# A streaming-encoder block on one core: up pairs 13, 15 and 17 in seven-product steps, the sums of x read on GpSimd's queue, and two edits at the ends of the up phases

## The chip, the cores and the metric

The kernel runs on one core of a Trainium2 chip. That core has five engines that work at once: TensorE (PE in the profile, with its weight loads as PEld), VectorE (DVE), ScalarE (ACT), GpSimd (POOL) and SyncE (SP). SP, ACT and POOL each have a queue for DMA transfers. The metric is the device time of one execution in microseconds; the median of several runs is compared.

## The reference

One layer of a hybrid encoder on x of 512 tokens by 1024 features, in float32. The change touches only the channel mixing part, the up and the down projection; in the reference it reads

```python
h = rms_norm(x, norm_ffn_g[l])
u = causal_dwconv(h @ w_up[l], conv_ffn_w[l])     # 1024 -> 2 x 2816, three taps
a, b = jnp.split(u, 2, axis=-1)
x = x + (jax.nn.silu(a) * b) @ w_down[l]          # 2816 -> 1024
```

In front of it stand the input projection, a gated convolution, attention with a forget gate, and their merge; behind it a last norm. None of these is changed.

## The kernel before

**Arithmetic.** TensorE multiplies numbers of a rounded kind. To keep float32's accuracy each factor is held as a high part, the rounded copy, and a low part, what the rounding left. A product is then three matmuls: high by high, low weight by high x, high weight by low x. The low parts of the weights are `wl`, the high ones `wh`; of activations the names are `x1h`/`x1l` (the input of the up projection, each 128 features by 512 tokens in eight blocks) and `gh`/`gl` (256 tokens wide, for everything that is summed first).

**Weights.** A list `stream` holds all weight chunks in the order of their use. For each chunk SP issues a load (L182) into one of four raw buffers, ACT copies it to `wh` (`split`, L275), DVE takes the difference `wl` (L279), and TensorE uses both. `wh` and `wl` have two buffers each, so the split of a chunk waits until TensorE is done with the chunk before the last. ACT and DVE run their instructions strictly in program order: whatever stands in front of a split delays it.

**Up pairs.** The 5632 columns of the up projection are 44 blocks of 128; block 2j and 2j + 1 are the pair j, the two factors of the gate. Pairs 0 to 11 are phase 0, 12 to 21 phase 1. A plain pair takes two chunks `up` and 96 matmuls. A pair in `SUP` is done with seven products instead of eight for each 2 x 2 block of blocks (Strassen's scheme in Winograd's form). It takes two steps; each has a chunk P (three products that use weights as they are, 18 matmuls) and a chunk F (four products with sums of weights, 24 matmuls). The sums of weights are formed in DRAM by DMA alone: SP copies (L208), POOL's queue adds with an accumulating DMA (L211). The sums of x lie in `gh`/`gl` too. In phase 0 DVE and ACT make them and store their float32 form to DRAM (`ys`). Since `gh`/`gl` hold other things at the end of phase 0, phase 1 reads that form back in four quarters y10 to y13 (`up_forms`: DMA at L1084, `gh` on ACT at L1076, `gl` on DVE at L1079). The tile `y` has one buffer: the read of a quarter is issued when the `gl` of the quarter before is done.

**Behind an up pair.** DVE multiplies the result by the norm (L1171), ACT and DVE apply the three taps (L566, L567, L570), ACT applies SiLU (L1231), POOL or DVE multiplies the two factors (`ge` for even pairs at L1236, `go` for odd ones), and after an odd pair DVE forms sums and ACT and DVE their high and low parts (L1262, L1263), the input of the down projection.

**Down steps.** At the end of each phase the down projection of that phase's pairs follows, again in seven-product steps (`STEPS`) with chunks P and F.

**What sets the order.** The Python program writes the engines' instructions in one order, and each engine keeps it. Work of ACT and DVE that may wait is put in a list `later`, each entry with the number of the chunk at whose split it is due, an estimate of its time, and tags ("e": evaluation of an up pair; "q": sums for the down steps). `split` ends with `run_later`, which writes out what is due, as far as its time fits; `flush_only` writes out everything with a tag at once. At the last pair of each phase `up` calls both.

Of the kernel before, what the change touches and what calls it, by code (L numbers as in the profile page):

```python
# [42 lines left out]
PHASES = ((0, 12), (12, NP))  # L43
# [4 lines left out]
STEPS = (  # L48
    tuple(((i, q), (i, q + 1)) for i, q in ((0, 0), (0, 2), (1, 0), (1, 2), (0, 4), (1, 4)))
    + tuple(((i, q), (i, q + 1)) for i in (3, 2) for q in (0, 2, 4)),  # L50
    (((2, 6), (2, 7)), ((2, 8), (2, 9)), ((0, 6), (0, 7)), ((0, 8), (2, 10)), ((0, 9), (0, 10)))
    + (((1, 6),), ((1, 7), (1, 8)), ((1, 9), (1, 10))),
)

# [3 lines left out]
PLAIN = [(m, k) for m in (6, 7) for k in range(*PHASES[1])]  # L58
PCUTS = (0, 8, 12, 20)

SUP = ((1, 2, 5), (14, 16))
XF = (26, 0)
UPD = tuple(tuple(((j, q), (j, q + 1)) for j in js for q in (0, 2)) for js in SUP)
DOUBLES = GATES + UPD[0] + STEPS[0] + UPD[1] + STEPS[1]
# [6 lines left out]
def block_kernel(ctx, tc, xT, vecs, wv, win, wmix, wo, wup, wst, wdp, outT):  # L71
# [3 lines left out]
    nc = tc.nc  # L75
# [6 lines left out]
    def keep(ins):  # L82
        return tc.keep_in_program_order(ins)
# [72 lines left out]
    later = []  # L156
# [638 lines left out]
    for i in range(n + LA):  # L795
# [8 lines left out]
        if 0 <= i - LA < n:  # L804
            pr, e, qb = units[i - LA]
# [249 lines left out]
    def up_forms(q, ph):  # L1055

        y = (gx if ph or q % 2 else hp).tile([P, 4, 2 * P], F32, tag="y", name=f"y{ph}{q}")
        b11, b12, b21, b22 = (y[:, i, :] for i in range(4))
        fs = slice(XF[ph] + 4 * q, XF[ph] + 4 * q + 4)

        def scale():
            for b in range(2):
                kb = 2 * q + b
                nc.scalar.activation(
                    y[:, 2 * b : 2 * b + 2, :], x1[:, kb, :].rearrange(halves_of, h=2), AF.Copy, scale=col(G2 + kb)
                )
            nc.vector.tensor_sub(b11, b11, b12)
            nc.vector.tensor_sub(b12, b22, b12)

        def sums():  # L1070
            nc.vector.scalar_tensor_tensor(b22, b11, -1.0, b22, op0=ALU.mult, op1=ALU.subtract)
            nc.vector.scalar_tensor_tensor(b21, b22, -1.0, b21, op0=ALU.mult, op1=ALU.subtract)


        def parts_of():
            nc.scalar.activation(gh[:, fs, :], y, AF.Copy)  # L1076
            if not ph:
                keep(nc.scalar.dma_start(ys[q], y))
            nc.vector.tensor_sub(gl[:, fs, :], y, gh.bitcast(F32)[:, fs, :])  # L1079
            if ph and q < 3:  # L1080
                up_forms(q + 1, ph)

        if ph:
            keep(nc.sync.dma_start(y, ys[q]))  # L1084
            due = [c[0] for c in stream].index(f"F{ND[0] + len(STEPS[0]) - 2}") + q
            later.append((due, 0.85, (("x", q),), parts_of))
            return
        for f, us in ((scale, 0.85), (sums, 0.85), (parts_of, 1.25)):
            later.append((0, us, (("x", q),), f))
# [51 lines left out]
    def up(j, ph, rb2, pu=None):  # L1141
        uu = []

        def tap(i, z):
            u = fp.tile([P, S], F32, tag="fu", name=f"fu{j}{i}", bufs=3)
            taps(u, z, CF + 3 * (2 * j + i))
            uu.append(u)

        if j in SUP[ph]:
            c = 2 * SUP[ph].index(j)  # L1150
            slot()
            seven(
                UPD[ph][c : c + 2], NU[ph] + c, {j: USETS[j]}, lambda q, g: up_form(ph, q, g), of="x",
                done=lambda i, banks, ids: merge(ph, j, banks, ids, rb2, tap, uu),
            )
            slot()
            return
        evacs = []
        for i in range(2):
            slot()  # L1160
            p = pu[i] if pu else block(f"up{2 * j + i}", x1h, x1l, True)
            if i and j + 1 == PHASES[ph][1]:
                split_next()
                if any(("e",) in w[2] for w in later):
                    flush_only((("e",),))
                    split()
            z = [None]

            def mul(i=i, p=p, z=z):
                z[0] = fp.tile([P, S], F32, tag="fz", name=f"fz{j}{i}", bufs=4)  # L1170
                nc.vector.tensor_mul(z[0], p, rb2)  # L1171

            evac = [(0.7, mul), (1.4, lambda i=i, z=z: tap(i, z[0]))]
            if i:
                evac.append((0, lambda: glu(ph, j, uu)))
            if any(("e",) in w[2] for w in later):
                later.extend((0, us, (("e",), acc.last) if x == 0 else (("e",),), f) for x, (us, f) in enumerate(evac))
            else:
                for _, f in evac:
                    f()  # L1180
# [46 lines left out]
    def glu(ph, j, uu):  # L1227
        a, b = uu
        q, k = j // 2, len(parts) - 1
        g0 = place(ph, q)  # L1230
        nc.scalar.activation(a, a, AF.Silu)  # L1231
        if j == NP - 1:
            nc.scalar.activation(tbl, a[: 4 * H, :1], AF.Sqrt, scale=0.0, bias=eps[: 4 * H])
        if j % 2 == 0:
            ge = glu.even = fp.tile([P, 2, 2 * P], F32, tag="ge", name=f"ge{q}", bufs=2)
            keep(nc.gpsimd.tensor_mul(ge, a.rearrange(halves_of, h=2), b.rearrange(halves_of, h=2)))  # L1236
            return
        flush_only([("q", x) for x in range(q)])
        ge = glu.even
        go = fp.tile([P, 6, 2 * P], F32, tag="gr", name=f"go{q}")  # L1240

        def mul(eng):
            return eng.tensor_mul(go[:, 0:2, :], a.rearrange(halves_of, h=2), b.rearrange(halves_of, h=2))

        if j + 1 < PHASES[ph][1]:
            keep(mul(nc.gpsimd))
        else:
            later.append((k + 3, 0.7, (("q", q),), lambda: mul(nc.vector)))
        b11, b12 = ge[:, 0, :], ge[:, 1, :]
        b21, b22, t1, t2, t3, t4 = (go[:, i, :] for i in range(6))  # L1250

        def t13():
            nc.vector.tensor_sub(t1, b11, b12)
            nc.vector.tensor_sub(t3, b22, b12)

        def t24():
            nc.vector.scalar_tensor_tensor(t2, t1, -1.0, b22, op0=ALU.mult, op1=ALU.subtract)
            nc.vector.scalar_tensor_tensor(t4, t2, -1.0, b21, op0=ALU.mult, op1=ALU.subtract)

        def hl(src, gs):  # L1260
            def f():
                nc.scalar.activation(gh[:, gs, :], src, AF.Copy)  # L1262
                nc.vector.tensor_sub(gl[:, gs, :], src, gh.bitcast(F32)[:, gs, :])  # L1263

            return f


        d = (2, 3, 4) if j + 1 < PHASES[ph][1] else (4, 5, 6)
        w = [(d[0], 0.85, t13), (d[0], 0.85, t24), (d[1], 0.7, hl(ge[:, : 1 + ph, :], slice(g0, g0 + 1 + NF * ph, NF)))]
        w += [(d[x > 0 and 2 or 1], 0.7, hl(go[:, x : x + 2, :], slice(g0 + 1 + x, g0 + 3 + x))) for x in (0, 4, 2)]  # L1270
        at = next((x for x, i in enumerate(later) if ("e",) in i[2]), len(later))
        later[at:at] = [(k + n, us, (("q", q),), f) for n, us, f in w]
# [49 lines left out]
    X, Y = (6, 7, 0, 1), (2, 3, 4, 5)  # L1322
    for ph, (j0, j1) in enumerate(PHASES):
        if ph:
            acc = turns(*(6, 7, 0, 1) * 4)
            make_forms(ND[1], len(DOUBLES), ph)
        for j in range(j0, j1):
            pu = None
# [208 lines left out]
```

## Time and profile before

| | |
|---|---|
| time, median of 3 runs | 694.92 us (694.84 to 695.49) |
| profiled execution | 694.18 us, of which the span of the trace is 692.4 us |
| granted TensorE clock, mean | 0.997 |
| phase 0, down steps | 465.8 to 523.8 us |
| phase 1, up pairs 12 to 21 | 523.8 to 631.1 us |
| phase 1, down steps | 631.1 to 667.8 us |
| plain end | to 692.4 us |

Stage bounds are the starts of the first matmuls of the stages in the timeline. A row of a timeline reads: start and duration in us, engine, line of the program, operation, what is written and read (buffer numbers left out), shape, count, and in brackets how long the engine stood idle before it and what ended the wait. A letter q behind an engine's name is its DMA queue.

### The profile page before, as it was taken

Reading aid. Unit: us, or ns where it says so; the run is one execution under the profiler, and the core shown is the slowest. Engines: PE = TensorE matmul, PEld = TensorE weight load, DVE = VectorE, ACT = ScalarE, POOL = GpSimd, SP = SyncE. Lnnn points to the kernel's source line nnn. Section 1 sums busy time; section 2 is a strip of 40 time slices with the busy share of each in tenths; the row PEclk is TensorE's granted clock in tenths of the full one; section 3 lists DMA queues with packets and bytes.
Section 4 is the critical chain, followed back from the end, with each engine's and each line's share of the span. In section 5 each row is a group of like instructions: output and inputs, shape, how many; then the busy total and the mean of one; then the engine's idle time right before and its main releaser. Section 6 shows DMA issues by size and latency. Waiting matters only on the chain. (4 is left out here: it accounts for less than half of the span.)

```text
span 692.4 us, 14690 instructions
## 1 busy us (share of the span) xinstructions
PE 683.1 (99%) x5936; PEld 680.6 (98%) x5936; DVE 554.2 (80%) x858; ACT 368.3 (53%) x579; POOL 190.5 (28%) x201
## 2 busy tenths in 40 slices
PE   9999999999999999999999999999999999999996
PEld 9999999999999999999999999999999999999995
DVE  6677787877578778769879699998787899988894
ACT  5675755554554444546554555545444544545572
POOL 6134947542020201214400144340100325231000
PEclk9999999999999999999999999999999999999998
DMA  8629999552568586788998498888945996676413
GB/s 308 225 67 293 216 243 204 134 120 92 185 144 221 166 268 205 230 308 213 158 313 241 126 233 222 200 242 231 252 149 167 337 231 157 188 168 182 154 31 122
DMA packets 65012, 137.53 MB, mean 199 GB/s; under 512 B 5760, under 2 KB 30352, under 8 KB 64688
## 3 DMA queue, kind: packets, MB, share of 16 engines
q1 hardware_dynamic: 44664, 107.28, 47.2%
q0 software_dynamic: 18464, 26.03, 23.4%
q10 hardware_dynamic: 1816, 3.29, 1.3%
q8 instruction: 46, 0.75, 0.4%
q14 instruction: 22, 0.18, 0.1%
HBM read 132.31 MB, written 47.71 MB: 260 GB/s over the span
## 5 line engine op out<-in xcount | busy, mean ns | idle before, releaser
L211 POOL DMA_DIRECT2D f<-in_wst_dram x66 | 77.7, 1371 | 27.1 <-DMA f<-f 26.8
L309 PE MATMUL p_up<-x1h,wh_up 128*128 128x256 f32 x416 | 81.2, 276 | 0.0
L309 PE MATMUL p_up<-x1l,wh_up 128*128 128x256 f32 x416 | 81.0, 276 | 0.0
L309 PE MATMUL p_up<-x1h,wl_up 128*128 128x256 f32 x416 | 81.0, 276 | 0.0
L279 DVE TENSOR_TENSOR wl_F<-raw_F,wh_F 128x1024 fp32r<-128x1024 f32 (+1 forms) x42 | 55.9, 1330 | 20.0 <-ACT wh_F L275 20.0
L275 ACT ACTIVATE wh_F<-raw_F 128x1024 fp32r<-128x1024 f32 (+1 forms) x42 | 44.3, 1054 | 39.5 <-PE dn L327 28.7
L309 PEld LDWEIGHTS p_up<-x1h,wh_up 128*128 128x128 f32 x416 | 62.7, 188 | 0.0
L309 PEld LDWEIGHTS p_up<-x1l,wh_up 128*128 128x128 f32 x416 | 62.7, 188 | 0.0
L309 PEld LDWEIGHTS p_up<-x1h,wl_up 128*128 128x128 f32 x416 | 62.6, 188 | 0.0
L309 PE MATMUL p_in<-xgh,wh_in 128*128 128x256 f32 x288 | 56.8, 279 | 0.0
L309 PE MATMUL p_in<-xgh,wl_in 128*128 128x256 f32 x288 | 56.6, 278 | 0.0
L309 PE MATMUL p_in<-xgl,wh_in 128*128 128x256 f32 x288 | 56.5, 278 | 0.0
L279 DVE TENSOR_TENSOR wl_P<-raw_P,wh_P 128x768 fp32r<-128x768 f32 (+1 forms) x42 | 41.7, 992 | 14.7 <-ACT wh_P L275 8.6
L327 PE MATMUL dn<-gh,wh_F 128*128 128x256 f32 x216 | 51.2, 277 | 1.2 <-ACT wh_F L275 1.2
L275 ACT ACTIVATE wh_P<-raw_P 128x768 fp32r<-128x768 f32 (+1 forms) x42 | 35.1, 835 | 32.1 <-PE dn L327 23.2
L327 PE MATMUL dn<-gl,wh_F 128*128 128x256 f32 x216 | 51.0, 276 | 0.0
L1236 POOL TENSOR_TENSOR ge<-fu,fu 128x512 f32<-128x512 f32 x11 | 20.1, 1831 | 110.5 <-DVE fu L570 85.6
L279 DVE TENSOR_TENSOR wl_up<-raw_up,wh_up 128x1024 fp32r<-128x1024 f32 x34 | 43.8, 1288 | 7.4 <-ACT wh_up L275 7.4
L275 ACT ACTIVATE wh_up<-raw_up 128x1024 fp32r<-128x1024 f32 x34 | 35.8, 1054 | 19.4 <-PE p_up L309 9.3
L309 PEld LDWEIGHTS p_in<-xgh,wh_in 128*128 128x128 f32 x288 | 44.7, 188 | 0.7
L309 PEld LDWEIGHTS p_in<-xgl,wh_in 128*128 128x128 f32 x288 | 43.7, 188 | 0.0
L309 PEld LDWEIGHTS p_in<-xgh,wl_in 128*128 128x128 f32 x288 | 43.6, 188 | 0.0
(343 smaller groups left out, 2211.8 us busy)
## 6 DMA issues: line engine op xcount, KB each, us to landing
raw_F<-f SPq DMA_DIRECT2D x41, 512.0 KB, 5.7
raw_up<-in_wup_dram SPq DMA_DIRECT2D x34, 512.0 KB, 5.6
raw_P<-in_wst_dram SPq DMA_DIRECT2D x41, 384.0 KB, 5.4
raw_in<-in_win_dram SPq DMA_DIRECT2D x24, 512.0 KB, 3.6
f<-in_wst_dram POOLq DMA_DIRECT2D x41, 256.0 KB, 6.8
f<-in_wst_dram SPq DMA_DIRECT2D x20, 512.0 KB, 7.1
f<-in_wst_dram POOLq DMA_DIRECT2D x20, 512.0 KB, 9.1
f<-f SPq DMA_DIRECT2D x40, 256.0 KB, 6.5
```

The source lines that it names most:

```text
L211: return lambda: keep(nc.gpsimd.dma_start(dst, src, accum_op=ALU.add))
L275: ins = nc.scalar.activation(hi, raw, AF.Copy)
L279: ins = nc.vector.tensor_sub(lo, raw, hi.bitcast(F32))
L309: keep(nc.tensor.matmul(out[:, cs], w, x[:, cs], start=start and i == 0 and c == 0, stop=stop and i == 2 and c == len(cut) - 1,))
L327: keep(nc.tensor.matmul(out, wl if x == 1 else wh, xl if x == 2 else xh, start=opens and bk not in seen, stop=closes and bk not in left,))
L1236: keep(nc.gpsimd.tensor_mul(ge, a.rearrange(halves_of, h=2), b.rearrange(halves_of, h=2)))
```

## The change

Pairs 13, 15 and 17 of phase 1 are done in seven-product steps in place of 14 and 16: one pair more, and all of them odd. The four reads of the sums of x go through POOL's queue in place of SP's. The down step of phase 1 that did positions (0, 8) and (2, 10) together is cut in two of one position each. At the last pair of each phase a split is now made always, and in front of what is flushed, where it was made behind it. The due numbers of the sums of a pair are one later if the next pair is a seven-product one, which concerns pair 1 alone. The turn of the PSUM banks of phase 1 follows.

```diff
@@ STEPS
-    (((2, 6), (2, 7)), ((2, 8), (2, 9)), ((0, 6), (0, 7)), ((0, 8), (2, 10)), ((0, 9), (0, 10)))
+    (((2, 6), (2, 7)), ((2, 8), (2, 9)), ((0, 6), (0, 7)), ((0, 8),), ((2, 10),), ((0, 9), (0, 10)))
@@
-SUP = ((1, 2, 5), (14, 16))
+SUP = ((1, 2, 5), (13, 15, 17))
@@ up_forms
         if ph:
-            keep(nc.sync.dma_start(y, ys[q]))
+            keep(nc.gpsimd.dma_start(y, ys[q]))
@@ up
             if i and j + 1 == PHASES[ph][1]:
                 split_next()
-                if any(("e",) in w[2] for w in later):
-                    flush_only((("e",),))
-                    split()
+                split()
+                flush_only((("e",),))
@@ glu
-        d = (2, 3, 4) if j + 1 < PHASES[ph][1] else (4, 5, 6)
+        d = (4, 5, 6) if j + 1 == PHASES[ph][1] else (3, 4, 5) if j + 1 in SUP[ph] else (2, 3, 4)
@@
-            acc = turns(*(6, 7, 0, 1) * 4)
+            acc = turns(*(6, 7, 0, 1) * 3, 6, 7)
```

Below, three places where the engines' order moves; names carry the numbers of chunks and quarters (`up24` and `up25` are pair 12, `P30`/`F30` the first seven-product step of phase 1), and line numbers behind L1163 are one lower in the changed program.

ACT's rows around the last reads of x, before:

```order
L1076 ACTIVATE gh_3988<-y11_6816 128x1024
L275 ACTIVATE wh_up24_6903<-raw_up24_6689 128x1024
L275 ACTIVATE wh_up25_6978<-raw_up25_6751 128x1024
L1282 ACTIVATE cz02_6909<-dn1824_6731 128x256
L1076 ACTIVATE gh_3988<-y12_6849 128x1024
L275 ACTIVATE wh_up26_7049<-raw_up26_6808 128x1024
L566 ACTIVATE fu120_6969<-fz120_6967,vec_64 128x512
L1076 ACTIVATE gh_3988<-y13_6877 128x1024
L1231 ACTIVATE fu120_6969<-fu120_6969 128x512
L275 ACTIVATE wh_up27_7114<-raw_up27_6869 128x1024
```

and in the changed program:

```order
L1076 ACTIVATE gh_3988<-y11_6825 128x1024
L275 ACTIVATE wh_up24_6914<-raw_up24_6695 128x1024
L275 ACTIVATE wh_up25_6988<-raw_up25_6757 128x1024
L1281 ACTIVATE cz02_6920<-dn1824_6737 128x256
L1076 ACTIVATE gh_3988<-y12_6858 128x1024
L275 ACTIVATE wh_P30_7057<-raw_P30_6815 128x768
L566 ACTIVATE fu120_6981<-fz120_6979,vec_64 128x512
L1076 ACTIVATE gh_3988<-y13_6888 128x1024
L1230 ACTIVATE fu120_6981<-fu120_6981 128x512
L275 ACTIVATE wh_F30_7089<-raw_F30_6817 128x1024
```

The reads keep their places; where the split of `up26` stood now stands that of `P30`, and behind the SiLU that of `F30` in place of `up27`.

The reads of x on SP's queue before, among the loads of weights:

```order
L182 DMA raw_up26_6808<-in_wup_dram 128x1024
L1084 DMA y11_6816<-ys_3993 128x1024
L1084 DMA y12_6849<-ys_3993 128x1024
L182 DMA raw_up27_6869<-in_wup_dram 128x1024
L1084 DMA y13_6877<-ys_3993 128x1024
L208 DMA f34_6912<-in_wst_dram 256x1x512
```

and on POOL's in the changed program:

```order
L211 DMA f34_4002<-in_wst_dram 256x1x256
L1084 DMA y11_6825<-ys_3993 128x1024
L1084 DMA y12_6858<-ys_3993 128x1024
L1084 DMA y13_6888<-ys_3993 128x1024
L1235 TENSOR_TENSOR ge6_7052<-fu120_6981,fu121_7047 128x512
```

On SP the loads no longer stand behind a read; on POOL the three reads stand behind the last addition to the weights' sums `f34` and in front of the product of pair 12.

DVE's rows around the first down step of phase 1 (chunk P34, F34 before, P36, F36 in the changed program), before:

```order
L1171 TENSOR_TENSOR fz211_8271<-p_up43_8214,rb_n2_4668 128x512
L279 TENSOR_TENSOR wl_F34_8305<-raw_F34_8065,wh_F34_8304 128x1024
L567 SCALAR_TENSOR_TENSOR fu211_8273<-fz211_8271,vec_64,fu211_8273 128x511
L279 TENSOR_TENSOR wl_P35_8335<-raw_P35_8134,wh_P35_8334 128x768
L570 SCALAR_TENSOR_TENSOR fu211_8273<-fz211_8271,vec_64,fu211_8273 128x510
```

and in the changed program:

```order
L1170 TENSOR_TENSOR fz211_8294<-p_up43_8221,rb_n2_4669 128x512
L279 TENSOR_TENSOR wl_F36_8285<-raw_F36_8057,wh_F36_8284 128x1024
L1262 TENSOR_TENSOR gl_3989<-ge9_8000,gh_3988 128x2x256
L567 SCALAR_TENSOR_TENSOR fu210_8290<-fz210_8219,vec_64,fu210_8290 128x511
L567 SCALAR_TENSOR_TENSOR fu211_8296<-fz211_8294,vec_64,fu211_8296 128x511
L570 SCALAR_TENSOR_TENSOR fu210_8290<-fz210_8219,vec_64,fu210_8290 128x510
L570 SCALAR_TENSOR_TENSOR fu211_8296<-fz211_8294,vec_64,fu211_8296 128x510
L1262 TENSOR_TENSOR gl_3989<-go9_8144,gh_3988 128x512 x3
L279 TENSOR_TENSOR wl_P37_8359<-raw_P37_8123,wh_P37_8358 128x768
```

Between the splits of the first F and the next P stand eight rows where one stood: the taps of both blocks of pair 21 and four low parts of the sums of pairs 18 and 19.

## The prediction

> **What bounds the kernel now.** I read the page's table of engines first, then the list of TensorE's waits, then the timelines of ACT, DVE and SP around the places where the change moves rows.
>
> ```profile
> span 692.4 us, 14690 instructions
> PE 683.1 (99%) x5936; PEld 680.6 (98%) x5936; DVE 554.2 (80%) x858; ACT 368.3 (53%) x579; POOL 190.5 (28%) x201
> ```
> ```profile
> engine line waited for: us in total, times, longest us
> PE dn L327 <- ACT wh_F L275: 1.2, 2, 0.7
> PE dn L327 <- DVE wl_F L279: 0.4, 1, 0.4
> PE p_up L327 <- DVE wl_up L279: 0.2, 1, 0.2
> ```
>
> TensorE is busy for 99% of the span; the four stalls listed are 1.8 us together. So a matmul taken away is time won, and every wait that is added in front of a matmul is time lost in full. The profiled run took 694.18 us, 0.74 under the median of the three timed ones (694.92). I make the sum against 694.18 and place the forecast between that basis and the median.
>
> **Term 1, fewer matmuls.** Pair 12 is a plain pair of 96 matmuls (2 blocks, 8 steps, 3 products, 2 halves). Its first matmul and the first of pair 13:
>
> ```profile
> 523.83 0.28 PE L327 MATMUL p_up<-x1h,wh_up 128*128 128x256 f32 x1
> 534.71 0.28 PE L327 MATMUL p_up<-x1h,wh_up 128*128 128x256 f32 x1
> ```
> 10.88 us / 96 = 0.1133 us each. A seven-product pair has 84, and one more pair becomes one: 12 x 0.1133 = **-1.36 us**. The step cut in two keeps its 42 matmuls.
>
> **Term 2, stalls of before that go.** The 0.4 us for wl_F is in pair 14, which becomes a plain pair:
>
> ```profile
> 554.72 0.38 PE L327 MATMUL dn<-x1h,wl_F 128*128 128x256 f32 x1 [0.35 <-DVE wl_F L279]
> ```
> In it and in the 0.2 us for wl_up, DVE was only just late, among rows whose order the change shifts. I take both as gone: **-0.6** (0 if they come back beside the new pairs).
>
> **Term 3, the chain of the y reads.** This is the term that decides. The tile y is single, so a read waits until gh and gl of the read before are made: four links, each a DMA, a copy on ACT, a difference on DVE. Before, its last three links were:
>
> ```profile
> 517.09 5.97 SPq L1084 DMA_DIRECT2D y<-ys  x2
> 529.61 0.32 SPq L1084 DMA_DIRECT2D y<-ys  x1
> ```
> ```profile
> 520.38 1.06 ACT L1076 ACTIVATE gh<-y 128x1024 fp32r<-128x1024 f32 x1 [0.95 <-DMA y<-ys]
> 521.35 1.04 ACT L275 ACTIVATE wh_up<-raw_up 128x1024 fp32r<-128x1024 f32 x1
> 527.26 1.06 ACT L1076 ACTIVATE gh<-y 128x1024 fp32r<-128x1024 f32 x1 [2.81 <-DMA y<-ys]
> 533.00 1.06 ACT L1076 ACTIVATE gh<-y 128x1024 fp32r<-128x1024 f32 x1 [1.73 <-DMA y<-ys]
> 536.62 1.05 ACT L275 ACTIVATE wh_up<-raw_up 128x1024 fp32r<-128x1024 f32 x1
> ```
> ```profile
> 522.61 1.22 DVE L279 TENSOR_TENSOR wl_up<-raw_up,wh_up 128x1024 fp32r<-128x1024 f32 x1
> ```
>
> ACT waited 0.95, 2.81 and 1.73 us for the reads and TensorE did not feel it: the weights queued behind them on ACT were those of plain pairs, wanted late. In the changed order the row behind the last gh<-y and the SiLU of pair 12 is wh_F30, the formed weights of pair 13's first step, and pair 13 comes one pair (10.88 us) before pair 14, which was the first of its kind.
>
> When is wh_F30 ready? Call the landing times of the three reads L1, L2, L3. The first can be issued at 517.09, as before. From gh's start to the next read's issue 529.61 - 527.26 = 2.35 us pass. From the last gh's start to the end of the split that stands behind the SiLU, 536.62 + 1.05 - 533.00 = 4.67 us pass (gl, a tap that waits behind gl on DVE, the SiLU, the split). Together 517.09 + 2 x 2.35 + 4.67 = 526.46, plus L1 + L2 + L3. TensorE wants it 18 matmuls into pair 13: 534.71 + 18 x 0.1133 = 536.75. So the stall is the sum of the three L less **10.3 us**, if positive. A part of it shows earlier: the splits of up24 stand behind gh<-y11 on ACT and gl on DVE and ended at 522.61 + 1.22 = 523.83, 3.45 after gh's start, where TensorE can begin on wh for 8 matmuls more (0.9 us); L1 over 523.83 + 0.9 - 3.45 - 517.09 = 4.2 us delays pair 12 itself.
>
> What is L on GpSimd's queue? The trace has no such read there. Its nearest rows, first the landing times (least, median, most) of the y reads on SP's queue, then those of the four reads of x at the start, of the same 512 KB on GpSimd's queue:
>
> ```profile
> DMA to landing us min/median/max: 3.3/3.9/4.5
> ```
> ```profile
> xt<-in_xT_dram POOLq DMA_DIRECT2D x4, 512.0 KB, 9.3
> DMA to landing us min/median/max: 6.6/9.3/12.0
> ```
> SP's own L were 3.3 (520.38 - 517.09), 3.4 (533.00 - 529.61) and the 4.5 in between: 11.2, which would stall 0.9 us. The lower bound is 3.3 each: 9.9, no stall. The upper one is 6.6 each, the quickest of the x reads: 19.8, a stall of 9.5. The x reads were issued together and shared the queue, the y reads come one at a time, so 9.3 and 12.0 do not apply; but the SP loads that the y reads held up before now run beside them. I take 5.0, the middle of 3.3 and 6.6: 15.0, **+4.7** (0 to +9.5), of which 0.8 falls at pair 12's start and the rest before pair 13's first formed product.
>
> The Trainium skill, "DMA: Bandwidth & Descriptors", section "SWDGE vs HWDGE vs iDMA", names about 1 us to the first byte on GpSimd's path against some 0.6 us on the other, and its fit in "Anatomy of one DMA" gives about 3.2 us for 512 KB; by that fit the stall would be nothing, by the first-byte figures about 2.1 us. The slowest-side rows above, 6.6 and more, disagree with the fit, under a heavier load than here.
>
> **Term 4, the end of phase 1.** Before, wh_F34 stood behind the SiLU of pair 21 and its table load:
>
> ```profile
> 630.54 0.63 ACT L1231 ACTIVATE fu<-fu 128x512 f32<-128x512 f32 x1 [2.15 <-DVE fu L570]
> 631.19 1.28 ACT L1233 ACT_TABLE_LOAD   x1
> 632.69 1.04 ACT L275 ACTIVATE wh_F<-raw_F 128x1024 fp32r<-128x1024 f32 x1
> ```
> ```profile
> 631.08 0.28 PE L327 MATMUL dn<-gh,wh_P 128*128 128x256 f32 x1
> 633.78 0.38 PE L327 MATMUL dn<-gh,wh_F 128*128 128x256 f32 x1 [0.50 <-ACT wh_F L275]
> ```
> ```profile
> 625.08 0.69 DVE L1263 TENSOR_TENSOR gl<-go,gh 128x512 fp32r<-128x512 f32 x1
> 625.68 0.74 DVE L570 SCALAR_TENSOR_TENSOR fu<-fz,vec,fu 128x510 f32<-128x510 f32 x1
> 633.76 1.23 DVE L279 TENSOR_TENSOR wl_F<-raw_F,wh_F 128x1024 fp32r<-128x1024 f32 x1 [1.79 <-ACT wh_F L275]
> 634.90 0.75 DVE L567 SCALAR_TENSOR_TENSOR fu<-fz,vec,fu 128x511 f32<-128x511 f32 x1
> 635.57 0.95 DVE L279 TENSOR_TENSOR wl_P<-raw_P,wh_P 128x768 fp32r<-128x768 f32 x1
> 636.44 0.74 DVE L570 SCALAR_TENSOR_TENSOR fu<-fz,vec,fu 128x510 f32<-128x510 f32 x1
> ```
> Now wh_F36 follows wh_P36 at once and needs only the buffer that TensorE gives back at the first step's start, S: the 0.50 us stall goes, **-0.5**. But what was flushed ahead of that split now stands behind it, and ahead of the next: between wl_F36 and wl_P37 DVE has four differences gl and four taps, where it had one tap. By the spacings of the rows a gl takes 625.68 - 625.08 = 0.60, a tap 635.57 - 634.90 = 0.67, wl_P 636.44 - 635.57 = 0.87, and wl_F ends 634.90 - 632.69 = 2.21 after wh_F's start. So wl_P37 is ready at S + 0.1 + 2.21 + 4 x 0.60 + 4 x 0.67 + 0.87 = S + 8.26. TensorE wants it after the first step's 42 matmuls (4.76) and 12 that use wh alone (1.36): S + 6.12. A new stall of **+2.1** (+2.8 if the eight rows take their full 0.69 and 0.75 instead of the spacings; nothing below, since DVE keeps its order, unless the rows stand ready earlier than TensorE's S by another stall before).
>
> **Term 5, the end of phase 0.** The same cut is made there, but wh_F18 still stands behind a SiLU that waits for DVE, so this stall stays:
>
> ```profile
> 466.99 0.63 ACT L1231 ACTIVATE fu<-fu 128x512 f32<-128x512 f32 x1 [0.89 <-DVE fu L570]
> 468.62 0.38 PE L327 MATMUL dn<-gh,wh_F 128*128 128x256 f32 x1 [0.66 <-ACT wh_F L275]
> ```
> ```profile
> 470.42 0.95 DVE L279 TENSOR_TENSOR wl_P<-raw_P,wh_P 128x768 fp32r<-128x768 f32 x1
> 471.29 0.74 DVE L570 SCALAR_TENSOR_TENSOR fu<-fz,vec,fu 128x510 f32<-128x510 f32 x1
> ```
> Two gl and a tap move in front of wl_P19: 471.29 + 2 x 0.60 + 0.67 = 473.16 against a need at 468.62 + 24 x 0.1133 + 1.36 = 472.70: **+0.4** (0 to +1).
>
> **Edits at nothing.** The down step cut in two has chunks of half the size, so its splits halve with its matmuls; the cover is the other step's 21 matmuls (2.4 us) against two splits of some 1.6 us on DVE, and without that cover 0.3 us. The later due numbers in phase 0 act on pair 1 alone, far from a stall. SP loses its three waits for y and issues weights sooner, which TensorE cannot use, since the splits wait for buffers. One more pair of formed weights adds additions on GpSimd's queue behind y10; if they hold up y11 it costs what L1 grows.
>
> **Sum:** -1.36 - 0.6 + 4.7 - 0.5 + 2.1 + 0.4 = +4.7, so 698.9 on the profiled run's basis and 699.7 on the median's. I forecast **699.4 us**.
>
> **Rivals.**
>
> *GpSimd's queue is about as quick as SP's here.* Reads come one at a time on a free queue; against it, no row on that queue is that quick. With L = 3.3 to 4.1 each the stall is 0 to 2.0, the sum 0.0 to +2.0 and the time 694.5 to 696.9. Chance 0.22, about half of it within the bounds of no change.
>
> *The clock drops in the stall.* The 3.9 us before pair 13's formed products would be over five times the longest wait listed above (0.7). At the kernel's end, behind TensorE's last matmul at 685.8, the windows (busy time of PE, PEld, DVE, ACT, POOL, then granted clock) show it halved 1.8 us later, and the first matmuls of the kernel, at a cold start, ran slowly:
>
> ```profile
> 685.80:687.60 1.80, 0.00 (x1) 0.00 (x0) 1.76 (x4) 0.00 (x0) 0.00 (x0) 1.00 0.21 73
> 687.60:692.40 4.80, 0.00 (x0) 0.00 (x0) 0.78 (x2) 0.00 (x0) 0.00 (x0) 0.50 0.55 195
> ```
> ```profile
> 1.05 4.11 PE L115 MATMUL warm<-ones 128*128 128x128 f32 x18 [1.05 <-DVE ones L107]
> ```
> If a cold stretch lasts those 4.1 us again at half speed it loses 2.0: 701.4. Against it: a stall split in two, or under 3 us, may not be seen by what sets the clock. Chance 0.22. The Trainium skill, "TensorE: Matmul & The Clock Gate", section "What's actually happening", has the clock decided over free-running windows of some 3.4 us; the trace's 1.8 us from the last matmul to the drop is within one such window, so whether a stall of 3.9 us is hit would hang on where the window lies.
>
> *The other side: faster.* The mechanism is SP's queue set free. It stood still in front of y reads, 5.97 us for two of them; with weights issued up to that much sooner, and the last row of the y chain early enough, nothing waits. It decides if each L is 3.4 us or less and if DVE is ahead of TensorE at the end of phase 1, so that the eight rows find their inputs before S. Then -1.36 - 0.6 - 0.5, 691.7 to 692.5. For it: ACT is half idle (53%). Against it: DVE cannot start the gl rows before wl_F36 in its order. Chance 0.12.
>
> *The change does not do what it says:* the counts of matmuls in program order differ by 12, so this is 0.02.
>
> **How the numbers follow.** My forecast has 0.36 (its own range 697.5 to 701), the quick queue 0.22, the clock 0.22, faster 0.12, no effect 0.02; the last 0.06 are reads of 6 us and more, 702 to 704.5. The range from 694.5 to 703.5 leaves out the faster case and the worst of the reads. A measurement here tells about 0.2% (1.4 us) from no change. Faster 0.12; within 0.2% 0.12, from half of the quick queue; slower 0.76.
>
> **What would show it.** Term 1: the count of PE matmuls 12 lower. Term 3: the landing time of y<-ys on GpSimd's queue near 5 us, gh<-y waiting on it, and a PE wait on wh_F of some 4 us in pair 13; a landing near 3.5 and no such wait would make the forecast wrong, and most likely too high. Term 4: a PE wait of about 2 us on wl_P at the second down step of phase 1, and none on wh_F at the first. Term 5: 0.4 us on wl_P at the second step of phase 0. The clock: a granted clock under 1.0 in a window just behind the stall in pair 13.

## The result, and the profile after

| | median | runs |
|---|---|---|
| before | 694.90 us | 694.32 to 695.49, 6 runs |
| changed | 697.88 us | 696.06 to 700.24, 6 runs |
| ratio | 1.0043 | 95% interval 1.0025 to 1.0060 |

The changed kernel is slower by 0.43%, 3.0 us. Its runs spread over 4.2 us, those of the kernel before over 1.2. The profiled execution took 697.25 us, 3.07 more than that of the kernel before. From the page, and from the list of TensorE's waits:

```profile
span 695.5 us, 14727 instructions
PE 683.1 (98%) x5924; PEld 680.6 (98%) x5924; DVE 561.8 (81%) x867; ACT 370.7 (53%) x584; POOL 194.8 (28%) x211
```
```profile
engine line waited for: us in total, times, longest us
PE dn L327 <- ACT wh_F L275: 3.3, 2, 2.6
PE dn L327 <- DVE wl_P L279: 1.1, 1, 1.1
PE dn L327 <- ACT wh_P L275: 0.4, 1, 0.4
```

The 12 matmuls are gone. The waits in the steps and pairs grew from 1.8 to 4.8 us, and they stand elsewhere: none at pair 14, none at a late wl_up. The places, in TensorE's timeline of the changed kernel (first formed product of the down steps of phase 0; first matmul of pair 12; first formed product of pair 13; first and second down step of phase 1):

```profile
469.17 0.39 PE L327 MATMUL dn<-gh,wh_F 128*128 128x256 f32 x1 [0.67 <-ACT wh_F L275]
524.96 0.28 PE L327 MATMUL p_up<-x1h,wh_up 128*128 128x256 f32 x1
540.79 0.39 PE L327 MATMUL dn<-x1h,wh_F 128*128 128x256 f32 x1 [2.63 <-ACT wh_F L275]
632.71 0.28 PE L327 MATMUL dn<-gh,wh_P 128*128 128x256 f32 x1
638.08 0.38 PE L327 MATMUL dn<-gh,wh_P 128*128 128x256 f32 x1 [0.44 <-ACT wh_P L275]
641.21 0.39 PE L327 MATMUL dn<-gh,wl_P 128*128 128x256 f32 x1 [1.08 <-DVE wl_P L279]
```

The chain that ends in the 2.63 us, in the timelines of GpSimd and of ACT:

```profile
518.49 0.58 POOL L1084 DMA_DIRECT2D y<-ys  x1 [16.97 <-DVE gl L1079]
524.99 0.55 POOL L1084 DMA_DIRECT2D y<-ys  x1 [5.93 <-DVE gl L1079]
532.45 0.53 POOL L1084 DMA_DIRECT2D y<-ys  x1 [6.90 <-DVE gl L1079]
```
```profile
522.37 1.07 ACT L1076 ACTIVATE gh<-y 128x1024 fp32r<-128x1024 f32 x1 [1.81 <-DMA y<-ys]
529.83 1.06 ACT L1076 ACTIVATE gh<-y 128x1024 fp32r<-128x1024 f32 x1 [4.23 <-DMA y<-ys]
536.09 1.06 ACT L1076 ACTIVATE gh<-y 128x1024 fp32r<-128x1024 f32 x1 [2.57 <-DMA y<-ys]
539.70 1.04 ACT L275 ACTIVATE wh_F<-raw_F 128x1024 fp32r<-128x1024 f32 x1
```

From the issue of a read to the start of its gh the three reads took 3.88, 4.84 and 3.64 us, 12.4 together. From gh's start to the next issue it is 2.62 us (524.99 - 522.37; 532.45 - 529.83), where SP needed 2.35 in the kernel before. The split behind the SiLU ends at 539.70 + 1.04 = 540.74, and TensorE goes on at 540.79.

The end of phase 1, in DVE's timeline:

```profile
634.01 1.23 DVE L279 TENSOR_TENSOR wl_F<-raw_F,wh_F 128x1024 fp32r<-128x1024 f32 x1
635.15 0.69 DVE L1262 TENSOR_TENSOR gl<-ge,gh 128x512 fp32r<-128x512 f32 x1
640.21 0.95 DVE L279 TENSOR_TENSOR wl_P<-raw_P,wh_P 128x768 fp32r<-128x768 f32 x1
641.08 1.22 DVE L279 TENSOR_TENSOR wl_F<-raw_F,wh_F 128x1024 fp32r<-128x1024 f32 x1
```

wl_P37 is ready at 641.08, 8.37 us behind the step's start at 632.71.

### The profile page after: what moved, and what is told of

Read it like the earlier page. It is cut to its first block, busy times and chain, and to the rows that moved or that the text cites. A ratio compares the mean times of both kernels' runs of the same rounds, so it can differ in the third digit from the quotient of the medians.

```text
span 695.5 us, 14727 instructions
## 1 busy us (share of the span) xinstructions
PE 683.1 (98%) x5924; PEld 680.6 (98%) x5924; DVE 561.8 (81%) x867; ACT 370.7 (53%) x584; POOL 194.8 (28%) x211
## 5 line engine op out<-in xcount | busy, mean ns | idle before, releaser
L211 POOL DMA_DIRECT2D f<-in_wst_dram x72 | 83.5, 1381 | 30.6 <-DMA f<-f 30.2
L309 PE MATMUL p_up<-x1l,wh_up 128*128 128x256 f32 x392 | 76.4, 276 | 0.0
L309 PE MATMUL p_up<-x1h,wh_up 128*128 128x256 f32 x392 | 76.4, 276 | 0.0
L309 PE MATMUL p_up<-x1h,wl_up 128*128 128x256 f32 x392 | 76.3, 276 | 0.0
L309 PEld LDWEIGHTS p_up<-x1l,wh_up 128*128 128x128 f32 x392 | 59.1, 188 | 0.0
L309 PEld LDWEIGHTS p_up<-x1h,wh_up 128*128 128x128 f32 x392 | 59.0, 188 | 0.0
L309 PEld LDWEIGHTS p_up<-x1h,wl_up 128*128 128x128 f32 x392 | 58.9, 188 | 0.0
L327 PE MATMUL dn<-gh,wh_F 128*128 128x256 f32 x228 | 54.2, 277 | 0.7 <-ACT wh_F L275 0.7
L327 PE MATMUL dn<-gl,wh_F 128*128 128x256 f32 x228 | 54.0, 276 | 0.0
L279 DVE TENSOR_TENSOR wl_P<-raw_P,wh_P 128x768 fp32r<-128x768 f32 (+1 forms) x45 | 43.8, 974 | 12.4 <-ACT wh_P L275 6.5
L327 PEld LDWEIGHTS dn<-gh,wh_F 128*128 128x128 f32 x228 | 42.8, 188 | 0.9 <-ACT wh_F L275 0.9
```

The lines of the kernel that those rows point to most:

```text
L211: return lambda: keep(nc.gpsimd.dma_start(dst, src, accum_op=ALU.add))
L279: ins = nc.vector.tensor_sub(lo, raw, hi.bitcast(F32))
L309: keep(nc.tensor.matmul(out[:, cs], w, x[:, cs], start=start and i == 0 and c == 0, stop=stop and i == 2 and c == len(cut) - 1,))
L327: keep(nc.tensor.matmul(out, wl if x == 1 else wh, xl if x == 2 else xh, start=opens and bk not in seen, stop=closes and bk not in left,))
```

## The experiments

Three groups were timed (e1, e2, e4, e5; e3, e6, e9, e10; e11, e12, e13, e15), each with runs of the kernel before on the same chip. The ratios are to those, and differences between kernels are taken from the ratios; by their intervals such a difference is known to 0.1 or 0.2%.

| | what | median | ratio, 95% |
|---|---|---|---|
| e1 | changed, y on SP | 695.31 | 1.0011 (1.0000 to 1.0023) |
| e2 | before, y on GpSimd | 698.51 | 1.0052 (1.0039 to 1.0065) |
| e4 | before, split first | 697.42 | 1.0033 (1.0021 to 1.0045) |
| e5 | before, pairs 13, 15, 17 | 699.58 | 1.0066 (1.0054 to 1.0078) |
| e3 | changed, flush first | 699.34 | 1.0051 (1.0035 to 1.0067) |
| e6 | changed, two buffers for y | 694.66 | 0.9992 (0.9983 to 1.0001) |
| e9 | e6, late taps | 694.83 | 0.9997 (0.9987 to 1.0007) |
| e10 | e6, y on SP | 693.51 | 0.9974 (0.9966 to 0.9982) |
| e11 | e10, late taps, other steps | 699.77 | 1.0073 (1.0059 to 1.0087) |
| e12 | e10, step whole | 695.97 | 1.0019 (1.0010 to 1.0027) |
| e13 | e10, flush first | 695.60 | 1.0010 (1.0002 to 1.0019) |
| e15 | changed, again | 697.79 | 1.0040 (1.0027 to 1.0052) |

### The y reads: e1, e6, e10, e2

e1, the changed kernel with one line back:

```diff
-            keep(nc.gpsimd.dma_start(y, ys[q]))
+            keep(nc.sync.dma_start(y, ys[q]))
```

> The changed kernel with the four y reads back on SP's queue. Theory (the stall before pair 13's first formed products is the length of the y chain, and GpSimd's queue made it longer): landings sum to about 11.2 us in place of 12.4 and a link has 2.35 us behind gh's start in place of 2.62, so TensorE's wait on wh_F30 falls from 2.7 to about 1.0 us and the time by 1.7 to 2, to about 696; the spread of the runs (696.1 to 700.2) shrinks, since the wait is too short for the clock. Rival 1 (SP set free was worth something): other loads come late, new waits, 697.9 or more. Rival 2 (the queue does not matter, the neighbours of pair 13 on DVE and ACT do): the wait stays at 2.5 or more.

The time fell by 0.32%, some 2.2 us, a little more than expected; the spread did not shrink (694.17 to 698.15). The reads, issued at 518.56, 524.22 and 531.73 us, took 3.3, 5.2 and 3.4 us until their gh began at 521.87, 529.38 and 535.17. That is 11.9 together, not the 11.2 that I expected, and in a second trace of the changed kernel (e15) the reads took 11.7 on GpSimd's queue. From gl of the first quarter to gl of the last the chain took 18.95 us in e1 (517.32 to 536.27) and 20.20 in the changed kernel (516.98 to 537.18). Of the 1.25 us between them 0.8 lie in the three ways from the gl that frees the tile to the next issue and the rest in the reads; the trace does not show where the rest of the 2.2 us was won. And the wait of pair 13 moved rather than fell. In TensorE's timeline and DVE's:

```profile
538.81 0.38 PE L327 MATMUL dn<-gh,wh_P 128*128 128x256 f32 x1 [2.01 <-DVE xm L1293]
```
```profile
536.27 1.23 DVE L1079 TENSOR_TENSOR gl<-y,gh 128x1024 fp32r<-128x1024 f32 x1 [1.78 <-ACT gh L1076]
538.07 0.68 DVE L1293 TENSOR_TENSOR xm<-xm,dn 128x512 f32<-128x512 f32 x1
```

The addition that frees a bank of PSUM for pair 13 now stood behind the last gl<-y on DVE (in the changed kernel it stands ahead of it). It is the same chain, ending one row away. The profile of e1 was of its longest run, and the windows (busy time of PE, PEld, DVE, ACT, POOL, then granted clock, DMA share and GB/s) show one reason why it was long:

```profile
538.00:540.00 2.00, 1.19 (x9) 1.19 (x10) 2.00 (x5) 1.59 (x3) 0.00 (x0) 0.92 1.01 371
540.00:542.00 2.00, 2.00 (x11) 2.00 (x11) 2.00 (x3) 1.45 (x2) 0.00 (x0) 0.50 1.03 415
542.00:544.00 2.00, 2.00 (x15) 2.00 (x15) 1.88 (x3) 0.00 (x0) 0.82 (x1) 0.72 0.56 225
```

Behind a wait of 2.01 us the clock was halved for 3.4 us (539.69 to 543.11): 11 matmuls in 2 us, where 20 stand in the window from 534 to 536.

e6 takes the chain away without touching the queue. The odd quarters are read into the tile of `go`, which is free at that time, so that a read is issued while the quarter before is still used:

```diff
-        y = (gx if ph or q % 2 else hp).tile([P, 4, 2 * P], F32, tag="y", name=f"y{ph}{q}")
+        if ph and q % 2:
+            y = fp.tile([P, 6, 2 * P], F32, tag="gr", name=f"y{ph}{q}")[:, :4, :]
+        else:
+            y = (gx if ph or q % 2 else hp).tile([P, 4, 2 * P], F32, tag="y", name=f"y{ph}{q}")
...
-            if ph and q < 3:
-                up_forms(q + 1, ph)
+            if ph and q < 2:
+                up_forms(q + 2, ph)
...
             later.append((due, 0.85, (("x", q),), parts_of))
+            if not q:
+                later.append((due - 4, 0, (("x", 1),), lambda: up_forms(1, 1)))
```

> The changed kernel with a second buffer for y (the odd quarters in the tile of go, free at that time): a read is issued while the quarter before is still used; still on GpSimd's queue. Theory: the chain of y no longer ends at pair 13, the wait on wh_F30 is gone (2.7 us and what the clock loses), 694.5 to 695.2, and the spread shrinks to that of the kernel before. Rival (wh_F30 is late for other reasons, ACT or DVE behind): a wait of 1 us or more stays, 696 or more.

As the theory had it: no wait on wh_F30, 0.51% less than the changed kernel, some 3.5 us. That is what the chain costs there, with whatever the clock takes behind the wait. In the two profiled runs, in which the clock was not lowered, the first formed product of pair 13 starts 2.1 us earlier (538.72 against 540.79). e10 is e6 with the reads on SP's queue.

> As e6 with the y reads on SP's queue. Theory (with two buffers the queue does not matter): the time of e6 within 0.4. Rival (SP blocked by a read delays weights): 1 us or more over e6.

SP's queue was better by 0.18%, 1.25 us, so both expectations missed: the queue does matter with two buffers, in the other direction from the rival. On GpSimd's queue the last read took 7.7 us, issued at 520.71 while the one before was still under way; its gh<-y began at 528.43, that of e10 at 523.82, and the weights of up25 stand behind it. By the starts of the matmuls e10 gains 0.6 us there, of 1.3 up to the last matmul. GpSimd's timeline and ACT's of e6, then ACT's of e10:

```profile
520.71 0.54 POOL L1087 DMA_DIRECT2D y<-ys  x1 [1.42 <-DVE gl L1082]
```

```profile
522.51 1.06 ACT L1079 ACTIVATE gh<-y 128x1024 fp32r<-128x1024 f32 x1 [1.74 <-DMA y<-ys]
528.43 1.06 ACT L1079 ACTIVATE gh<-y 128x1024 fp32r<-128x1024 f32 x1 [3.91 <-DMA y<-ys]
```
```profile
521.21 1.06 ACT L1079 ACTIVATE gh<-y 128x1024 fp32r<-128x1024 f32 x1 [0.87 <-DMA y<-ys]
523.82 1.06 ACT L1079 ACTIVATE gh<-y 128x1024 fp32r<-128x1024 f32 x1 [0.59 <-DMA y<-ys]
```

e10 is the best version of the study, faster than both kernels: 0.9974 (0.9966 to 0.9982), 1.8 us under the kernel before.

e2 puts the reads of the kernel before on GpSimd's queue, with the line of e1 the other way round.

> The kernel before with the y reads on GpSimd's queue and nothing else. Theory: the reads take about 1.9 us longer as a chain, but the weights behind the last read are those of a plain pair's second block, wanted about 3 us after they are ready, so the time stays at 694.9 within 0.4 and TensorE shows no new wait over 0.4. Rival (reads on GpSimd's queue cost by themselves): 1.5 to 2 us slower.

A miss: 3.6 us slower. The reads took 13.8 us together (3.97, 4.32, 5.51). I had taken the slack behind the last read to be 3 us; TensorE wants wh of that block at its start, which leaves 540.15 - 537.67 = 2.5 in the trace of before. The chain came 3.3 us later (the split ends at 540.99) and DVE, once late, stayed late into pair 14. By the starts of the matmuls the three places lose 2.7 of the 3.4 us of this trace:

```profile
541.05 0.39 PE L327 MATMUL p_up<-x1h,wh_up 128*128 128x256 f32 x1 [0.50 <-ACT wh_up L275]
549.63 0.39 PE L327 MATMUL dn<-x1h,wh_F 128*128 128x256 f32 x1 [0.45 <-ACT wh_F L275]
557.44 0.38 PE L327 MATMUL dn<-x1h,wl_F 128*128 128x256 f32 x1 [0.95 <-DVE wl_F L279]
```

So the mechanism is the chain in this kernel too; what I had wrong is how much room it had.

### The pairs alone, and the two edits at the phase ends: e5, e4, e3, e13, e12

e5 has of the change only the pairs:

```diff
-SUP = ((1, 2, 5), (14, 16))
+SUP = ((1, 2, 5), (13, 15, 17))
...
-            acc = turns(*(6, 7, 0, 1) * 4)
+            acc = turns(*(6, 7, 0, 1) * 3, 6, 7)
```

> The kernel before with pairs 13, 15, 17 in seven-product steps (and the turn of the banks that goes with it), nothing else. Theory: 12 matmuls fewer -1.4, the waits at pair 14 and at a late wl_up -0.8, a wait of about 1.0 on wh_F30 (chain of y on SP's queue) and of about 1.9 on wl_P37: 695.6 (695 to 696.5). Rival (the loss lies in the other edits): 692.7.

A miss by 4 us: the pairs alone are slower than the whole change. The waits:

```profile
PE dn L327 <- ACT wh_F L275: 3.6, 2, 3.0
PE dn L327 <- DVE xm L1294: 2.2, 1, 2.2
PE dn L327 <- DVE gl L1263: 1.4, 1, 1.4
```

The 2.2 us are the y chain, ending on the PSUM bank as in e1. The 3.0 us are wh_F36: DVE comes to the end of phase 1 with more left to do (from 600 us to the down steps it is never idle for more than 0.24 us at a time; in the kernel before it is for 0.5 to 1.5 us five times), so the SiLU of pair 21 begins late, and the table load and wh_F36 stand behind it on ACT:

```profile
633.78 0.63 ACT L1231 ACTIVATE fu<-fu 128x512 f32<-128x512 f32 x1 [3.66 <-DVE fu L570]
634.43 1.28 ACT L1233 ACT_TABLE_LOAD   x1
635.92 1.04 ACT L275 ACTIVATE wh_F<-raw_F 128x1024 fp32r<-128x1024 f32 x1
```

I put that down to pair 17, the latest of the three, but no run shows which pair does it. The 1.4 us are the low parts of position 10 in the step ((0, 8), (2, 10)). So each of the two other edits removes a wait that the pairs make.

e4 is the kernel before with the moved split alone:

```diff
                 split_next()
-                if any(("e",) in w[2] for w in later):
-                    flush_only((("e",),))
-                    split()
+                split()
+                flush_only((("e",),))
```

> The kernel before with the split put in front of the flush at the last pair of each phase, and nothing else. Theory (the eight rows in front of wl of the second down step come from the later evaluation of pairs 17 to 20, not from the moved split): the wait on wh_F34 (0.7) goes, a wait of 0.3 on wl_P19 comes, none over 0.3 on wl_P35: 694.5. Rival (the moved split itself puts the rows there): a wait of about 2 us on wl_P35, 696 to 697.

2.3 us slower, and neither theory had the place. There is no such wait on wl_P35, so the moved split does not put the eight rows there; the 0.3 on wl_P19 came; the wait on wh_F34 stayed; and a new one of 1.4 us stands at the whole step, since what is flushed later gives its sums later:

```profile
PE dn L327 <- DVE gl L1262: 1.4, 1, 1.4
PE dn L327 <- ACT wh_F L275: 1.2, 2, 0.7
...
PE dn L327 <- DVE wl_P L279: 0.3, 1, 0.3
```

e3 and e13 undo the moved split, in the changed kernel and in e10 (the diff of e4 the other way round).

> The changed kernel with flush and split at the last pair of each phase as before. Theory: the wait of 0.3 on wl_P19 goes, a wait of some 0.6 on wh_F36 comes back, the wait on wl_P37 stays near 2: no change within the spread, 697 to 698.5. Rival (the moved split put the eight rows there): 2 us less, about 695.9.

> e10 with flush and split at the last pair of each phase as in the kernel before. Theory (the moved split trades a wait of 3.1 us on wh_F36 for one of about 1.5 more on wh_P37 and wl_P37): 1 to 2.5 us slower than e10, 694.5 to 696. Rival (the moved split costs more than it brings): faster than e10, 692 to 693.

e3 was 0.08% above the changed kernel, within the spread. On the quieter e10 the effect shows: e13 is slower than e10 by 0.36%, 2.5 us, as its theory had it. The wait of e13, and the windows behind it:

```profile
634.13 0.58 PE L327 MATMUL dn<-gh,wh_F 128*128 128x256 f32 x1 [2.94 <-ACT wh_F L275]
```
```profile
634.00:636.00 2.00, 1.86 (x8) 1.87 (x9) 1.89 (x3) 2.00 (x5) 0.00 (x0) 0.51 0.00 0
636.00:638.00 2.00, 2.00 (x13) 2.00 (x13) 2.00 (x4) 1.72 (x4) 0.00 (x0) 0.64 0.40 131
```

Here the halved clock costs less than it seems: the slow matmuls give DVE the time that it needs for wl_P37, on which nothing waits then. Against e10 the matmuls are 2.6 us late at this wait, 4.1 us late at 637 us, and only 2.0 us late at the low weights of the second step.

e12 leaves the down step whole in e10:

```diff
-    (((2, 6), (2, 7)), ((2, 8), (2, 9)), ((0, 6), (0, 7)), ((0, 8),), ((2, 10),), ((0, 9), (0, 10)))
+    (((2, 6), (2, 7)), ((2, 8), (2, 9)), ((0, 6), (0, 7)), ((0, 8), (2, 10)), ((0, 9), (0, 10)))
```

> e10 (two buffers for y, SP's queue) with the down step ((0, 8), (2, 10)) left whole. Theory (dividing it makes room for the sums of position 10, which a whole step wants too early; e4 and e5 showed 1.4 us of wait there): a wait of 1 to 2 us on gl in the fourth step, 694.5 to 695.5. Rival (dividing costs and brings nothing): the time of e10, 693.5.

0.45% slower, the theory's side, with its wait in the fourth step:

```profile
649.70 0.39 PE L327 MATMUL dn<-gl,wh_P 128*128 128x256 f32 x1 [1.36 <-DVE gl L1267]
```

Dividing the step gives the sums of position 10 another 21 matmuls of time. The wait is 1.36 us (1.8 by the starts of the matmuls) and the time by ratio some 3; of the rest 0.6 lie behind the last matmul, and I have no cause for it.

### Trying to remove the wait at the second down step: e9, e11

e9 is e6 without the flush at the end of phase 1; the taps of pair 21 come where they fit, at the latest behind the split of the second step's F.

```diff
                 split()
-                flush_only((("e",),))
+                if not ph:
+                    flush_only((("e",),))
...
-        flush_only((("e",),))
+        if not ph:
+            flush_only((("e",),))
         seven(
...
             flush(wants[name])
+            if of == "q" and n == 3:
+                flush_only((("e",),))
```

> As e6, and the taps of pair 21 are not written out before the down steps of phase 1, but as they fit behind its first two. Theory: the rows in front of wl_P37 shrink to the four gl, the wait of 2 us on wh_P37 and wl_P37 falls under 0.8: 692.5 to 693.5, faster than both kernels. Rival (DVE is too full there, the work only moves): a wait of like size at the third to fifth step, 694.5 or more.

The rival's case: nothing waits on wh_P37 or wl_P37, and 1.5 us of waits stand at position 10:

```profile
PE dn L327 <- DVE gl L1270: 1.5, 3, 0.7
```

e11 adds SP's queue and asks for position 10 later, by pairing (0, 8) with (0, 9) and (2, 10) with (0, 10) in `STEPS`.

> Two buffers for y, reads on SP's queue, the late taps of e9, and the positions of the fourth and fifth down steps of phase 1 in another order, (0, 8) with (0, 9) and (2, 10) with (0, 10), so that position 10 is wanted 21 matmuls (2.4 us) later. Theory (in e9 the DVE work only moved to the sums of position 10, which are 2.4 us late there): most of the waits of e9 and the wait on wl_P37 are gone, 691.5 to 692.7. Rival (DVE is full through these steps and the lateness follows wherever position 10 goes): waits of 2 us in all, 693.5.

Worse than either theory. The 1.4 us stay, and a new wait is the largest of all:

```profile
PE dn L327 <- DVE cz L1290: 3.7, 1, 3.7
PE dn L327 <- DVE gl L1270: 1.4, 1, 1.4
```

With the positions paired so, the sums of both output halves 0 and 2 end in the same step. DVE works off the first before the second, and the next step needs the banks of the second. Behind the wait the clock was halved for 3.4 us (660.29 to 663.71), which is a part of the loss. This wait was of my making; it says nothing of the change.

### The changed kernel again: e15

> The changed kernel again, beside the others on the same chip, for more runs and a second profile. Theory (a wait of 2.8 us or more in front of pair 13's formed products, and in some executions a lowered clock behind it): median 697 to 699, single runs between 696 and 701, the lower clocks (0.994 to 0.996) in the longer ones; if this profile falls on such a run, the granted clock is about 0.5 in the windows just behind that wait. Rival (the longer runs come from longer reads alone): the long runs have the clock of the short ones.

1.0040, as before. Of its five runs the two shorter ones (696.36, 696.42) have a granted clock of 0.998 and 0.997, the three longer ones (697.79 to 698.46) 0.996. In the first six runs, 0.994 to 0.996 went with 698.5 to 700.2 and 0.998 with 696.1 to 697.3. That leans towards the lowered clock as a cause of the long runs, and no more. The mean over a run also holds its end: in every trace the clock is halved for the last 1.7 to 5.5 us, behind the last matmul, and this alone brings the mean of e4 to 0.996. Only 0.994 and 0.995 lie below that. And both profiles of the changed kernel fell on runs whose clock was not lowered (waits of 2.63 and 2.0 us on wh_F30, none lowered behind), so a lowered clock behind a wait is shown only in e1, e3, e5, e11 and e13, not in the changed kernel itself.

## Why the prediction was right

It forecast 699.4 us, slower than before; 697.88 came, from the places that it named. The last column takes the two profiled runs and compares how long TensorE took from one place to the next, by the starts of its matmuls; it counts what a wait costs also where the list of waits does not show it.

| term | predicted | listed | by the starts of the matmuls |
|---|---|---|---|
| 1, matmuls | -1.36 | 12 fewer in the page | -1.36 |
| 2, waits at pair 14 and wl_up | -0.6 | both gone: -0.6 | -1.05 (pair 13's formed products to the down steps: 91.92 us, before 94.33; less term 1) |
| 3, y chain | +4.7 | wait of 2.63; 3.5 by e6 | +2.9 (pair 12 to pair 13's formed products: 15.83 us, before 12.92) |
| 4, wh_F of the first step | -0.5 | gone: -0.5 | both together +1.5 (down steps of phase 1 to the end: 62.79 us, before 61.32) |
| 4, wl_P of the second step | +2.1 | 0.44 + 1.08 = +1.5 | |
| 5, end of phase 0 | +0.4 | none; 0.3 in e4 | +0.6 (first formed product of the down steps of phase 0 to pair 12: 55.79 us, before 55.21) |

**Term 3** had the mechanism and the place right and the size too large, and this is the main error. The reads took 4.1 us in the mean (12.4 / 3) where I took 5.0, the middle between SP's 3.3 and the 6.6 of the x reads at the start: the x reads were no measure, having been issued together. A second error went the other way: I gave a link 2.35 us behind gh's start, as on SP; on GpSimd's queue it is 2.62, and the first read is issued late by the same 0.27. With the measured reads and these three 0.27 the term's sum is 4.7 - 2.6 + 0.8 = 2.9, which is what the starts of the matmuls show. In the timed runs e6 gives 3.5; the difference would be what the clock takes in the longer runs, which no trace of the changed kernel shows.

By the first-byte figures of the Trainium skill, "DMA: Bandwidth & Descriptors", section "Specifications" (the prediction names another section of that page for them), the sum of the reads would have been 12.4, an estimate (11.2 + 3 x 0.4) with which the profile agrees (12.4; 11.7 in e15). The fit of the Trainium skill, "DMA: Bandwidth & Descriptors", section "Anatomy of one DMA", gives an estimate of about 3.2 us for 512 KB, which is under every read measured in the changed kernel (3.5 to 4.8 us).

**Term 4** was right in both halves: wl_P37 was ready 8.37 us behind the step's start, 8.26 forecast. TensorE lists 1.5 and not 2.1 us of waits there because wh_P37 came late too, which shifted the need; the low weights were wanted at 632.71 + 6.12 = 638.83 and used at 641.21, so 2.4 us were lost there. What I had not seen is why the eight rows are there. I put them down to the moved split; e4 and e13 show that the split, moved alone, brings no wait there, and that without it the end of phase 1 costs 2.5 us more. Six of the eight rows, the four gl and two taps, stand there in e5 too, where the pairs are all that was changed. So the pairs bring them; the moved split adds two taps.

**Edits at nothing.** For the step cut in two my cover held, but 'nothing' was the wrong comparison: the step left whole would have cost 0.45% in e12. For the sum it makes no difference, since the forecast was for the changed kernel as a whole; for an engineer who undoes edits one by one it does. Freed SP brought nothing that shows, as said: e1 with SP blocked again is the faster kernel. The additions on GpSimd's queue did not hold up y11 either: GpSimd had stood idle for 16.97 us when it issued the read. The later due numbers of pair 1 were not run alone.

**Rivals.** The quick queue was nearer than I gave it: L of 3.6 and 3.9 in two of three reads, 4.8 in the third, and their sum of 12.4 is that rival's upper end (3 x 4.1). It was to end at 696.9; in the profiled run the longer links (0.8) and the 0.55 us below, which no sum had, make up what lies beyond. So the wait on wh_F in pair 13 bears out the mechanism, while the size of the reads lies between the forecast and this rival. The lowered clock is real in other kernels of the study; that it makes the spread of the changed kernel is likely and not shown. Faster by a freed SP did not happen.

**What is left over.** 0.55 us of the 3.07 lie ahead of the down steps of phase 0 (469.17 in place of 468.62 with the same wait) and no term has them. In the changed kernel they arise in the first 9 us, where the matmuls change later from the slow to the quick pace. TensorE's timeline there, of the kernel before and of the changed one:

```profile
5.53 0.39 PE L479 MATMUL pb<-wh_v,xgh 128*128 128x256 f32 x2
```
```profile
5.50 0.63 PE L479 MATMUL pb<-wh_v,xgh 128*128 128x256 f32 x2
```

All ten kernels profiled with the new pairs come to the down steps of phase 0 later than the kernel before by 0.3 to 0.9 us, and the two without them (e2, e4) do not. The late change of pace is not the whole of it: in e5, e11 and e12 the quick pace begins about as early as in the kernel before, and TensorE waits 0.6 to 0.7 us for wh_v instead. The cause stays open.

Nothing else is left: 0.55 + 0.58 + 2.91 - 1.36 - 1.05 + 1.47 = 3.10, the difference of the spans (695.5 - 692.4). The listed waits (3.0 more) and the matmuls (-1.36) fall 0.9 us short of that beside the 0.55, since matmuls next to a wait also start late without one being listed, as at wl_P19.

## What to carry to other kernels

A read-back into a single buffer is a chain: what it costs is not the landing time but the sum over all its links against the first consumer that stands behind the last one, and moving that consumer one stage forward can turn slack into a stall without a line of the chain being touched. Where engines keep program order, edits at a stage's end are worth what the others leave: here the pairs alone lost 4.6 us, the moved split alone 2.3, and inside the best version the split won 2.5; judge them in the version that is to stay. The larger part of the cure was a second buffer for the chain (0.51%); the queue back on SP won 0.18% beside it.

## What the runs showed of the hardware

A wait of TensorE as short as 2.01 us was followed by a halved clock (e1: granted 0.50 at 540 to 542), while one of 2.63 us in the changed kernel was not. The traces' records of the granted clock show what told the two apart. In the five traces with a lowered stretch inside (e1, e3, e5, e11, e13) it lasted 3.41 us each time, and it began a whole number of such lengths behind the clock's first rise (e1: 7.21 to 539.69 us, 156 of them). Cut each run into these lengths, and what counts is TensorE's idle time within one of them. The five largest of all 14 traces, up to the last matmul, and the five next:

| idle in us within one length, clock halved behind it | idle in us within one length, clock not halved |
|---|---|
| 2.98 (e11, of a wait of 3.71) | 1.58 (e3, of a wait of 2.93) |
| 2.82 (e13, of 2.94) | 1.48 (e15, of 1.99) |
| 2.38 (e5, of 2.96) | 1.40 (changed kernel, of 2.63) |
| 2.01 (e1, of 2.01) | 1.39 (e3, of 3.28, the first part) |
| 1.90 (e3, of 3.28, the second part) | 1.36 (e11 and e12, of 1.36) |

The wait of 2.63 us was cut in two at 539.57 us; that of e1 lay whole in one length. In these traces the line runs between 1.58 and 1.90 us, and where a wait falls on this grid differs from run to run: the first rise of the clock came at 3.9 to 7.2 us.

The Trainium skill, "TensorE: Matmul & The Clock Gate", section "What's actually happening", has free-running windows of some 3.4 us, so that a wait's place in the window matters and not its length alone; these runs agree with that, and a wait well under 3.4 us is enough.

Reads of 512 KB issued singly took 3.5 to 5.5 us on GpSimd's queue (changed kernel, e15, e2, e3) and 3.2 to 5.6 us on SP's (before, e1, e4, e5), from issue to gh. The three of a trace add to 11.7 to 13.8 us on the one and 10.5 to 12.1 on the other, 0.4 us more per read in the mean on GpSimd's queue. From gh's start to the next issue GpSimd's queue needed 0.27 us more (2.62 against 2.35).
